# Three arms of an expert put in another order, with the group work moved into them

## The chip, the cores and the metric

The kernel runs on one core of a Trainium2 chip. The metric is the device time of one execution in microseconds (us), the median of the timed runs. Five engines run side by side, each through its own stream of instructions: PE multiplies matrices, DVE and ACT do element-wise work, POOL is little used here, and SP issues the weight transfers. Instructions stream to an engine from memory; the page lists these fetches as DMA queues of their own, of the kind "instruction".

## The reference, cut to what matters

One layer of an encoder, 256 tokens and 16 meta tokens of width 1024. A mixer (SSD and differential attention) comes first; it ends some 380 us into the execution, and the change does not touch it. Then a routed feed-forward: each of 256 tokens picks 4 of 32 experts.

```python
logits = xf @ w_router + b_router
top_val, top_idx = lax.top_k(logits, TOP_K)          # 4 of 32
gates = softmax(top_val)
# for every expert e, on the tokens that picked it:
hidden = xb @ w_gate_up[e] + b_gate_up[e]            # 1024 x 2048
gate, up = min(hidden[:D], 7), clip(hidden[D:], -7, 7)
y = gate * sigmoid(1.702 * gate) * (up + 1) @ w_down[e] + b_down[e]   # 1024 x 1024
out = segment_sum(y * gate_of_slot, slot_token)
```

Each expert has 12 MB of weights in float32, and all 32 are read: 384 MB. How many tokens an expert has depends on the data.

## The kernel before, in words

**The weight ring.** `load_page` (L1002 to L1010) brings weights in pages of 1 MB into a ring of 19 buffers (`NS`): 8 pages of `w_gate_up` and 4 of `w_down` for an expert. SP issues them. `follow(e, k)` stands behind the last use of a page and issues the page 19 places further on, so a transfer can start only when PE has done with the page in its buffer.

**An expert.** The tokens of an expert lie in slots, 32 to a part: A holds slots 0 to 31, B 32 to 63, C 64 to 95, D 96 to 127. For a part PE runs the up part (`up32`, bias at L1096, weights at L1098, into `pA` to `pD`), DVE and ACT apply the activation (`act`), PE turns the result (`turn`, L1117, `atA`), and PE runs the down part (`down32`, L1130, `dA`), whose result `place` copies to `yrow` (L1138, L1140). Parts A and B read gathered tokens from `w1`, in which four experts (a group, `GE`) lie side by side; C and D are gathered for one expert from a one-hot matrix `eo` that `pick` makes on DVE (L1045).

**The arms.** The number of tokens `n` of an expert is a register value (`counts`, L1183, loaded on each engine), and every engine branches on it. `arms` writes three arms for each of the 32 experts, unrolled: a heavy one for n > 64 (gather, A, B, and within it a further branch at L1199 on n > 96 for C alone or C and D, then `combine` into the sums `acc`, L1169), a middle one for n > 32 (A and B) and a light one (A alone). The compare is at L1192 (n > 32) and L1193 (n > 64). An engine that leaves an arm jumps over the arms behind it to the next expert; this jump is recorded with the line of its `If` (L1193 for the heavy and the middle arm).

**The hint.** `tell` marks, inside expert e, on PE alone, which way the branch labelled `x{e+1}` of the next expert will go.

**Group work.** Behind the last expert of a group, outside the arms, `gather_group` gathers the tokens of the next group into `w1` (L1055, `xg`), and for each of parts A and B `combine` adds `yrow` to the sums (L1169, `acc`) and `slots` makes the placement matrices `pgb` of the next group (L1078, L1080, `ptA` and `ptB`). All of `mark` is the start of the sums, in expert 0.

The order on PE, DVE, ACT and SP is as written (`manual_schedule`).

Of the kernel before, what the change touches and what calls it, by code (L numbers as in the profile page):

```python
# [9 lines left out]
F32 = mybir.dt.float32  # L10
# [7 lines left out]
ET = mybir.EngineType  # L18
# [29 lines left out]
def hybrid_trunk_kernel(  # L48
# [974 lines left out]
    oh = ext[:, 512:1024].rearrange("p (b s) -> p b s", b=NB)  # L1023
    bdn, yx = ext[0:NE, 1024:2048], ext[0:64, 1024:2048]
    nc.scalar.dma_start(bdn, b_down[0])
    w1 = pg.tile([128, 2, KD, 128], F32, tag="d1", name="w1")
    pgb = [[cp.tile([128, 128], F32, name=f"pgb{i}{b}", tag=t) for b, t in enumerate(ts)]
           for i, ts in enumerate((("m1", "tri"), ("pgb10", "pgb11")))]
    pgx = cp.tile([128, NB, 128], F32, tag="pb", name="pgx")[0:64]
# [8 lines left out]
                                iota[:, None, ES * i:ES * i + ES].to_broadcast([128, GE, ES]),  # L1038
                                posm[:, b, g * GE:(g + 1) * GE, None].to_broadcast([128, GE, ES]), ALU.is_equal)

    def pick(e, off, name):

        eo = wk.tile([128, NB, 64], F32, tag="sd", name=f"eo{name}")
        for b in range(NB):
            V.tensor_scalar(eo[:, b, :], iota[:, 0:64], float(off), posm[:, b, e:e + 1], ALU.add, ALU.is_equal)  # L1045
        return eo

    def gather_group(name, ks, raw=False):

# [92 lines left out]
    def ups(e, parts, last):  # L1142

        p = [wps([128, 2, 256], f"p{pt[4]}") for pt in parts]
        for k in range(KD):
            for pt, q in zip(parts, p):
                up32(e, k, weights(e, k), q, pt[0])
            if last:
                follow(e, k)
        for pt, q in zip(parts, p):  # L1150
            act(q, pt[1], wk.tile([128, 256], F32, tag="sd", name=f"th{pt[4]}"))
# [30 lines left out]
    def counts(e):  # L1182
        return nc.values_load(cnt[0:1, e:e + 1], engines=(ET.PE, ET.DVE, ET.Activation, ET.SP), min_val=0, max_val=S)  # L1183

    def arms(e, n, mark, tell):

        r0 = ES * (e % GE)
        pa = (w1[:, 0, :, r0:r0 + ES], 0, yrow[:, 0], r0, f"A{e}")
        pb_ = (w1[:, 1, :, r0:r0 + ES], 512, yrow[:, 1], r0, f"B{e}")
        pc = (xTx[:, :, 0:32], 1024, yx, 0, f"C{e}")  # L1190
        pd_ = (xTx[:, :, 32:64], 1536, yx, 32, f"D{e}")
        with tc.If(n > 32, label=f"x{e}") as c1:  # L1192
            with tc.If(n > 64) as c2:  # L1193
                eo = pick(e, 64, f"{e}")
                gather(eo, f"x{e}")
                slots(eo, slice(e, e + 1), pgx, f"x{e}")
                ups(e, [pa, pb_], False)
                tell()
                with tc.If(n > 96) as c3:  # L1199
                    ups(e, [pc, pd_], True)  # L1200
                    mark()
                    downs(e, [pa, pb_], False)
                    downs(e, [pc, pd_], True)
                with c3.Else():
                    ups(e, [pc], True)
                    mark()
                    downs(e, [pa, pb_], False)
                    downs(e, [pc], True)
                combine(pgx, yx)
            with c2.Else():  # L1210
                tell()
                ups(e, [pa, pb_], True)
                mark()
                downs(e, [pa, pb_], True)
        with c1.Else():
            tell()
            ups(e, [pa], True)
            mark()
            downs(e, [pa], True)

    front[0] = False
    for i in range(NS):
# [3 lines left out]
    with tc.manual_schedule(engines={ET.PE, ET.DVE, ET.Activation, ET.SP}):  # L1226
        gather_group("0", range(0, 8, 2), raw=True)
        cts[0] = counts(0)
        gates()
        for E, b in ((V, 0), (G, 1)):  # L1230
            E.tensor_mul(h1[:, b, :], h1[:, b, :], gb1[:, 0, :])
            E.tensor_add(h1[:, b, :], h1[:, b, :], gb1[:, 1, :])
        hd = page("d2", [2 * D], F32, "hd")
        for e in range(NE):
            g, el = divmod(e, GE)
            if e + 1 < NE:
                cts[e + 1] = counts(e + 1)
            n = cts.pop(e)
            m = cts.get(e + 1)
            if el == GE - 1 and e + 1 < NE:  # L1240
                pick_group(g + 1)
            if e + 1 == NE:
                A.activation(gsum, ident[:, 0:NB], AF.Sqrt)
                gb2 = slot[NE * PE_ % NS]
                nc.gpsimd.dma_start(gb2[:, 0, :], row_bc(ln2_g, D))  # L1245
                nc.gpsimd.dma_start(gb2[:, 1, :], row_bc(ln2_b, D))

            def mark(m=m, e=e):
                if e == 0:
                    start_acc()  # L1250
                    V.memset(yx, 0.0)

            def tell(m=m, e=e):
                if m is not None:
                    tc.mark_branch_hint_location(f"x{e + 1}", hint=m > 32, engines=[ET.PE])

            arms(e, n, mark, tell)
            if el == GE - 1 and e + 1 < NE:
                gather_group(f"{g + 1}", range(0, 8, 2))
            if el == GE - 1 and e + 1 < NE or e == 0:  # L1260
                for i in range(2):
                    if e:
                        combine(pgb[i], yrow[:, i])
                    h = g + 1 if e else 0
                    slots(oh[:, :, 128 * i:128 * i + 128], slice(h * GE, (h + 1) * GE), pgb[i], f"{'AB'[i]}{h}")
        combine(pgb[1], yrow[:, 1])


# [46 lines left out]
    with c.Else():  # L1315
        combine(pgb[0], yrow[:, 0])
        for e in range(NE):
            with tc.If(nc.values_load(cnt[0:1, e:e + 1], min_val=0, max_val=S) > 128):
                for k in range(PE_):
                    load_page(e * PE_ + k, (NE * PE_ + 1 + k) % NS)  # L1320
                for off in (128, 192):
                    nm = f"{e}o{off}"
                    eo = pick(e, off, nm)
                    gather(eo, f"x{nm}")
                    slots(eo, slice(e, e + 1), pgx, f"x{nm}")
                    p = [wps([128, 2, 256], f"p{nm}{i}") for i in range(2)]
# [49 lines left out]
```

## Time and profile before

| | us |
|---|---|
| median of 3 runs (1479.12 to 1482.28) | 1479.97 |
| the profiled execution | 1474.79 |
| its span, first to last instruction | 1472.7 |
| PE busy with matmuls | 1185.7 |
| DVE busy | 426.1 |
| ACT busy | 294.6 |

The span is given in 40 slices of 36.8 us in the page. The experts take the time from 393 to 1452 us. With this data the 32 experts take the following arms, read off the timeline of PE (L light, M middle, H heavy; a bar between groups of four):

L L L L | H L H M | M L L H | L L M L | L L L L | H L L M | L M L M | L M H L

That is 20 light ones, 7 middle ones and 5 heavy ones; one of the heavy ones (expert 11) has all four parts, the others three.

### The profile page before, as it was taken

What the parts mean: (1) busy time and instruction counts of PE and PEld (TensorE: products, weight loads), DVE (VectorE), ACT (ScalarE), POOL (GpSimd) and SP (SyncE); (2) the same over time, 40 slices, a digit from 0 to 9 for tenths busy, and PEclk for the clock granted to TensorE, in tenths of its full rate; (3) what the DMA queues carried; (4) which work ended last, traced back from release to release, by engine and by line L of the source; (5) the groups of instructions that cost most, each with busy time, mean ns of one, the idle gap of its engine ahead of it and who ended that gap; (6) DMA issues with size and microseconds to landing.
All of it is one profiled execution on the core that took longest, in us unless ns stands there. A gap on an engine that the chain in (4) does not pass through costs nothing. (4 is left out here: it accounts for less than half of the span.)

```text
span 1472.7 us, 24271 instructions
## 1 busy us (share of the span) xinstructions
PE 1185.7 (81%) x10294; PEld 727.6 (49%) x10294; DVE 426.1 (29%) x940; ACT 294.6 (20%) x630; POOL 83.0 (6%) x65
## 2 busy tenths in 40 slices
PE   5899999899777968688697976856976777787875
PEld 5799999889532533344243533411532443242432
DVE  5976765456411110211112012011021111111113
ACT  4454475454300100001000100100100010010011
POOL 5422400000100000000000000000000000000001
PEclk9999999999888999989888889977898898899888
DMA  6465673768499998877998399999998999999740
GB/s 170 133 168 125 153 185 106 225 200 332 182 405 417 418 412 354 347 301 302 377 418 325 151 416 418 415 418 418 419 382 350 416 417 416 417 416 414 307 174 31
DMA packets 101982, 458.40 MB, mean 311 GB/s; under 512 B 8626, under 2 KB 49739, under 8 KB 52635
## 3 DMA queue, kind: packets, MB, share of 16 engines
q1 hardware_dynamic: 100554, 451.59, 79.2%
q0 software_dynamic: 800, 3.03, 0.7%
q8 instruction: 146, 2.39, 0.7%
q10 hardware_dynamic: 400, 0.73, 0.2%
q14 instruction: 82, 0.66, 0.1%
HBM read 454.27 MB, written 1.05 MB: 309 GB/s over the span
## 5 line engine op out<-in xcount | busy, mean ns | idle before, releaser
L1098 PE MATMUL pA<-ring,w 128*32 128x512 f32 x2048 | 294.3, 664 | 21.7 <-DMA ring<-in_w_gate_up_dram 21.1
L1098 PEld LDWEIGHTS pA<-ring,w 128*32 128x32 f32 x2048 | 91.9, 120 | 170.9 <-issue 112.4
L1130 PE MATMUL dA<-ring,hd 128*32 128x256 f32 x2048 | 150.9, 443 | 17.4 <-ACT hd L1118 14.5
L1103 DVE TENSOR_SCALAR hd<-pA 128x256 f32<-128x256 f32 x32 | 13.6, 425 | 449.5 <-PE pA L1098 322.2
L1098 PE MATMUL pB<-ring,w 128*32 128x512 f32 x768 | 116.2, 618 | 0.0
L1130 PEld LDWEIGHTS dA<-ring,hd 128*32 128x32 f32 x2048 | 72.3, 126 | 79.8 <-issue 26.0
L1105 ACT ACTIVATE thA<-hd 128x256 f32<-128x256 f32 x32 | 13.3, 416 | 468.6 <-DVE hd L1103 455.0
L1140 DVE COPY yrow<-dA 32x256 f32<-32x256 f32 x96 | 40.4, 420 | 216.1 <-PE dA L1130 153.5
L1096 PE MATMUL pA<-bgt,sel 96*32 96x256 bf16 x256 | 19.4, 337 | 99.6 <-issue 93.2
L1096 PEld LDWEIGHTS <-sel 96*32 96x32 bf16 x400 | 12.8, 104 | 138.5 <-issue 124.5
L1055 PE MATMUL xg<-ext,hh 128*128 128x256 f32 x256 | 63.5, 410 | 8.7 <-issue 4.5
L1055 PEld LDWEIGHTS xg<-ext,hh 128*128 128x128 f32 x256 | 52.1, 206 | 21.2 <-issue 7.8
L1169 PE MATMUL acc<-yrow,pgb 128*128 128x512 f32 x128 | 58.1, 598 | 1.0 <-DVE yrow L1140 1.0
L1245 POOL DMA_DIRECT2D ring<-in_ln_g_dram x1 | 0.6, 574 | 1018.5 <-PE dB L1130 1018.5
L1098 PEld LDWEIGHTS pB<-ring,w 128*32 128x32 f32 x768 | 33.0, 116 | 46.9 <-issue 46.8
L1117 PE MATMUL atA<-ident,hd 128*128 128x128 f32 x64 | 16.0, 334 | 47.4 <-DVE hd L1111 47.4
L1138 ACT COPY yrow<-dA 32x256 f32<-32x256 f32 x32 | 11.6, 363 | 200.2 <-DVE yrow L1140 153.9
L1130 PE MATMUL dB<-ring,hd 128*32 128x256 f32 x768 | 51.6, 387 | 0.0
L1117 PEld LDWEIGHTS atA<-ident,hd 128*128 128x128 f32 x64 | 10.1, 207 | 78.2 <-issue 61.5
L1098 PE MATMUL pC<-ring,ext 128*32 128x512 f32 x320 | 39.7, 612 | 0.6 <-issue 0.6
L162 PE MATMUL xbc<-hTh,wh_xbc 128*128 128x272 f32 x128 | 38.2, 300 | 0.0
L163 PE MATMUL xbc<-hTl,wh_xbc 128*128 128x272 f32 x128 | 37.8, 296 | 0.0
(523 smaller groups left out, 2120.3 us busy)
## 6 DMA issues: line engine op xcount, KB each, us to landing
ring<-in_w_gate_up_dram SPq DMA_DIRECT2D x256, 1024.0 KB, 19.9
ring<-in_w_down_dram SPq DMA_DIRECT2D x127, 1024.0 KB, 19.5
wr_xbc<-in_w_in_dram SPq DMA_DIRECT2D x8, 1024.0 KB, 10.5
wr_g<-in_w_in_dram SPq DMA_DIRECT2D x8, 1024.0 KB
wr_z<-in_w_in_dram SPq DMA_DIRECT2D x4, 1024.0 KB
wr_k<-in_w_in_dram SPq DMA_DIRECT2D x4, 1024.0 KB, 10.9
wr_v<-in_w_in_dram SPq DMA_DIRECT2D x4, 1024.0 KB
wr_q<-in_w_in_dram SPq DMA_DIRECT2D x4, 1024.0 KB, 13.7
```

The source lines that it names most:

```text
L162: TE.matmul(p, wh, xh, start=first, stop=False)
L163: TE.matmul(p, wh, xl, start=False, stop=False)
L1055: TE.matmul(p[:, j, :], h1[:, b, k * 128:(k + 1) * 128], oh[:, b, :], start=b == 0, stop=b == 1)
L1096: TE.matmul(o[:, u, :], sel[:, e:e + 1].to_broadcast([96, 32]), bgt[u][:, 256 * j:256 * j + 256], start=u == 0, stop=False)
L1098: TE.matmul(o, x[:, k, :], w[:, :, 256 * j:256 * j + 256], start=False, stop=k == KD - 1)
L1103: V.tensor_scalar(gg, p[:, 0, :], 7.0, None, ALU.min)
L1105: A.activation(t, gg, AF.Tanh, scale=0.851)
L1117: TE.transpose(p[:, t, :], hd[:, co + 256 + t:co + 512:2], ident)
L1130: TE.matmul(p[j * 32:(j + 1) * 32, :], at[:, t, k * 32:(k + 1) * 32], w[:, t, j * 256:(j + 1) * 256], start=k == 0 and t == 0, stop=k == 3 ...
L1138: A.copy(o, p[r0:r0 + 32, :])
L1140: V.tensor_copy(o, p[j * 32:j * 32 + 32, :])
L1169: TE.matmul(ap[b][n], w[b], y[:, n * 512:(n + 1) * 512], start=False, stop=stop)
```

## The change

The light arm stands first under `If(n <= 32)`, the middle one next under `If(n <= 64)`, and the heavy one last. The hint tells `m <= 32` in place of `m > 32`. `mark` becomes `fill`, at the same place between the up and the down part; it now also holds the group work, `gather_group` in the last expert of a group, and `combine` and `slots` in the first expert of the next one. `pick(e, 64)` is called for every expert ahead of the branch, and its result `eo` lies in the page of `w1`, of which 128 elements behind the tokens are set apart.

```diff
--- before.py
+++ after.py
@@ -1023,7 +1023,9 @@
     oh = ext[:, 512:1024].rearrange("p (b s) -> p b s", b=NB)
     bdn, yx = ext[0:NE, 1024:2048], ext[0:64, 1024:2048]
     nc.scalar.dma_start(bdn, b_down[0])
-    w1 = pg.tile([128, 2, KD, 128], F32, tag="d1", name="w1")
+    w1 = pg.tile([128, KD * T], F32, tag="d1", name="w1")
+    eo = w1[:, 2 * D:2 * D + 128].rearrange("p (b s) -> p b s", b=NB)
+    w1 = w1[:, 0:2 * D].rearrange("p (i k s) -> p i k s", i=2, k=KD)
     pgb = [[cp.tile([128, 128], F32, name=f"pgb{i}{b}", tag=t) for b, t in enumerate(ts)]
            for i, ts in enumerate((("m1", "tri"), ("pgb10", "pgb11")))]
     pgx = cp.tile([128, NB, 128], F32, tag="pb", name="pgx")[0:64]
@@ -1038,12 +1040,10 @@
                                 iota[:, None, ES * i:ES * i + ES].to_broadcast([128, GE, ES]),
                                 posm[:, b, g * GE:(g + 1) * GE, None].to_broadcast([128, GE, ES]), ALU.is_equal)
 
-    def pick(e, off, name):
-
-        eo = wk.tile([128, NB, 64], F32, tag="sd", name=f"eo{name}")
+    def pick(e, off):
+
         for b in range(NB):
             V.tensor_scalar(eo[:, b, :], iota[:, 0:64], float(off), posm[:, b, e:e + 1], ALU.add, ALU.is_equal)
-        return eo
 
     def gather_group(name, ks, raw=False):
 
@@ -1182,41 +1182,41 @@
     def counts(e):
         return nc.values_load(cnt[0:1, e:e + 1], engines=(ET.PE, ET.DVE, ET.Activation, ET.SP), min_val=0, max_val=S)
 
-    def arms(e, n, mark, tell):
+    def arms(e, n, fill, tell):
 
         r0 = ES * (e % GE)
         pa = (w1[:, 0, :, r0:r0 + ES], 0, yrow[:, 0], r0, f"A{e}")
         pb_ = (w1[:, 1, :, r0:r0 + ES], 512, yrow[:, 1], r0, f"B{e}")
         pc = (xTx[:, :, 0:32], 1024, yx, 0, f"C{e}")
         pd_ = (xTx[:, :, 32:64], 1536, yx, 32, f"D{e}")
-        with tc.If(n > 32, label=f"x{e}") as c1:
-            with tc.If(n > 64) as c2:
-                eo = pick(e, 64, f"{e}")
+        pick(e, 64)
+        with tc.If(n <= 32, label=f"x{e}") as c1:
+            tell()
+            ups(e, [pa], True)
+            fill()
+            downs(e, [pa], True)
+        with c1.Else():
+            with tc.If(n <= 64) as c2:
+                tell()
+                ups(e, [pa, pb_], True)
+                fill()
+                downs(e, [pa, pb_], True)
+            with c2.Else():
                 gather(eo, f"x{e}")
                 slots(eo, slice(e, e + 1), pgx, f"x{e}")
                 ups(e, [pa, pb_], False)
                 tell()
                 with tc.If(n > 96) as c3:
                     ups(e, [pc, pd_], True)
-                    mark()
+                    fill()
                     downs(e, [pa, pb_], False)
                     downs(e, [pc, pd_], True)
                 with c3.Else():
                     ups(e, [pc], True)
-                    mark()
+                    fill()
                     downs(e, [pa, pb_], False)
                     downs(e, [pc], True)
                 combine(pgx, yx)
-            with c2.Else():
-                tell()
-                ups(e, [pa, pb_], True)
-                mark()
-                downs(e, [pa, pb_], True)
-        with c1.Else():
-            tell()
-            ups(e, [pa], True)
-            mark()
-            downs(e, [pa], True)
 
     front[0] = False
     for i in range(NS):
@@ -1245,24 +1245,23 @@
                 nc.gpsimd.dma_start(gb2[:, 0, :], row_bc(ln2_g, D))
                 nc.gpsimd.dma_start(gb2[:, 1, :], row_bc(ln2_b, D))
 
-            def mark(m=m, e=e):
+            def fill(e=e, g=g, el=el):
                 if e == 0:
                     start_acc()
                     V.memset(yx, 0.0)
+                if el == 0:
+                    for i in range(2):
+                        if e:
+                            combine(pgb[i], yrow[:, i])
+                        slots(oh[:, :, 128 * i:128 * i + 128], slice(g * GE, (g + 1) * GE), pgb[i], f"{'AB'[i]}{g}")
+                if el == GE - 1 and e + 1 < NE:
+                    gather_group(f"{g + 1}", range(0, 8, 2))
 
             def tell(m=m, e=e):
                 if m is not None:
-                    tc.mark_branch_hint_location(f"x{e + 1}", hint=m > 32, engines=[ET.PE])
-
-            arms(e, n, mark, tell)
-            if el == GE - 1 and e + 1 < NE:
-                gather_group(f"{g + 1}", range(0, 8, 2))
-            if el == GE - 1 and e + 1 < NE or e == 0:
-                for i in range(2):
-                    if e:
-                        combine(pgb[i], yrow[:, i])
-                    h = g + 1 if e else 0
-                    slots(oh[:, :, 128 * i:128 * i + 128], slice(h * GE, (h + 1) * GE), pgb[i], f"{'AB'[i]}{h}")
+                    tc.mark_branch_hint_location(f"x{e + 1}", hint=m <= 32, engines=[ET.PE])
+
+            arms(e, n, fill, tell)
         combine(pgb[1], yrow[:, 1])
 
 
@@ -1320,7 +1319,7 @@
                     load_page(e * PE_ + k, (NE * PE_ + 1 + k) % NS)
                 for off in (128, 192):
                     nm = f"{e}o{off}"
-                    eo = pick(e, off, nm)
+                    pick(e, off)
                     gather(eo, f"x{nm}")
                     slots(eo, slice(e, e + 1), pgx, f"x{nm}")
                     p = [wps([128, 2, 256], f"p{nm}{i}") for i in range(2)]
```

PE at the end of the light arm of expert 1. In these rows dA is the down part, a ring buffer holds a page, sel and bgt are the bias of the next up part, and cnt holds the token counts. Before, the light arm is the last of the three, and the load of a count (each expert loads the count of the one behind it) and the compares of expert 2 (L1192, L1193) stand right behind it, then its heavy arm:

```order
L1130 MATMUL dA_5796<-ring_3900,hd 32x256 x8
L1192 UNCONDITIONAL_BRANCH
L1183 TENSOR_LOAD cnt
L1192 COMPARE_AND_BRANCH
L1193 COMPARE_AND_BRANCH
L1070 MATMUL xgx_5855<-eo_5852,hh 128x64 x16
```

Now the same place of expert 1, the end of its light arm:

```order
L1130 MATMUL dA_5081<-ring_3900,hd 32x256 x8
L1193 UNCONDITIONAL_BRANCH
L1199 COMPARE_AND_BRANCH
L1262 REGISTER_ALU
L1371 BRANCH_PREFETCH_HINT
L1096 LDWEIGHTS sel
L1096 MATMUL pA_5126<-bgt_3324,sel 32x256
```

Behind the light arm stand now the compare that opens the other two arms (L1199) and the middle arm; the jump of L1193 leads past both to the count and the compare at which expert 2 begins.

PE at the end of the heavy arm of expert 1 (acc are the sums, pgx the placement of C and D). Before, the middle arm follows:

```order
L1169 MATMUL acc_3891<-ext,pgx 128x512
L1193 UNCONDITIONAL_BRANCH
L1255 REGISTER_ALU
L1372 BRANCH_PREFETCH_HINT
L1096 LDWEIGHTS sel
```

Now the next expert follows, with the load of a count, its one compare and its light arm:

```order
L1169 MATMUL acc_3891<-ext,pgx 128x512
L1199 UNCONDITIONAL_BRANCH
L1183 TENSOR_LOAD cnt
L1193 COMPARE_AND_BRANCH
L1262 REGISTER_ALU
L1371 BRANCH_PREFETCH_HINT
L1096 LDWEIGHTS sel
```

So the arm that ends next to the following expert is now the heavy one and no longer the light one.

PE in the light arm of expert 3, the last of the first group, between its up part (pA) and its down part (dA), as it is now:

```order
L1098 MATMUL pA_6810<-ring_3902,w_3882 32x512 x4
L1055 MATMUL xg_6865<-ext,hh 128x256 x4
L1055 MATMUL xg_6871<-ext,hh 128x256 x4
L1055 MATMUL xg_6877<-ext,hh 128x256 x4
L1055 MATMUL xg_6883<-ext,hh 128x256 x4
L1117 MATMUL atA_6889<-ident,hd 128x128 x2
```

The four rows of xg stood behind the arms before; they are now between the last up matmul and the turn, and each of the three arms holds a copy of them.

## Rows read from the trace of the kernel before

**Rows 1.** the page, whole execution: DMA rate in 40 slices, PE's code fetches

```profile
GB/s 170 133 168 125 153 185 106 225 200 332 182 405 417 418 412 354 347 301 302 377 418 325 151 416 418 415 418 418 419 382 350 416 417 416 417 416 414 307 174 31
...
q8 instruction: 146, 2.39, 0.7%
```

**Rows 2.** who PE waited for, whole execution: us in total, times, longest us

```profile
PE pA L1096 <- issue: 93.2, 16, 10.6
PE atA L1117 <- DVE hd L1111: 47.4, 26, 2.9
PE pA L1098 <- DMA ring<-in_w_gate_up_dram: 21.1, 21, 1.5
PE xgx L1070 <- DVE eo L1045: 10.4, 5, 3.1
PE atB L1117 <- DVE hd L1111: 8.0, 7, 1.5
PE pA L1096 <- DVE yrow L1140: 5.9, 4, 2.3
...
PE xg L1055 <- issue: 4.5, 2, 3.2
...
PE xg L1055 <- ACT yrow L1138: 3.1, 3, 1.0
```

**Rows 3.** timeline of PE where experts meet: start us, us, what, idle before

```profile
554.73 0.68 PE L1096 MATMUL pA<-bgt,sel 96*32 96x256 bf16 x8 [9.41 <-issue]
...
567.03 3.66 PE L1130 MATMUL dA<-ring,hd 128*32 128x256 f32 x64 [0.51 <-ACT hd L1118]
...
858.19 5.35 PE L1130 MATMUL dA<-ring,hd 128*32 128x256 f32 x64 [0.51 <-ACT hd L1118]
868.84 0.68 PE L1096 MATMUL pA<-bgt,sel 96*32 96x256 bf16 x8 [5.31 <-issue]
869.22 2.01 PE L1098 MATMUL pA<-ring,w 128*32 128x512 f32 x8
...
902.52 0.68 PE L1096 MATMUL pA<-bgt,sel 96*32 96x256 bf16 x8 [6.72 <-issue]
```

**Rows 4.** branches of PE's sequencer, single ones: ns min/median/max, start us

```profile
L1192 PEldq COMPARE_BRANCH  x1: 3577/3577/3577, 437.3 to 437.3; - x1
...
L1193 PEldq COMPARE_BRANCH  x1: 6061/6061/6061, 542.5 to 542.5; - x1
...
L1193 PEldq COMPARE_BRANCH  x1: 6257/6257/6257, 862.1 to 862.1; - x1
...
L1192 PEldq COMPARE_BRANCH  x1: 354/354/354, 1001.4 to 1001.4; - x1
...
L1193 PEldq COMPARE_BRANCH  x1: 1744/1744/1744, 1242.1 to 1242.1; - x1
...
L1192 PEldq COMPARE_BRANCH  x1: 5564/5564/5564, 1244.3 to 1244.3; - x1
...
L1193 PEldq COMPARE_BRANCH  x1: 3610/3610/3610, 1422.1 to 1422.1; - x1
```

**Rows 5.** windows around two such branches: busy by engine, PEclk, DMA share, GB/s

```profile
862.00:868.00 6.00, 1.53 (x24) 0.67 (x16) 1.26 (x3) 0.36 (x1) 0.00 (x0) 0.78 1.01 414
...
1422.00:1429.00 7.00, 2.94 (x7) 1.06 (x6) 0.03 (x1) 0.19 (x1) 0.00 (x0) 0.77 0.02 5
```

**Rows 6.** timeline of PE: starts of experts 12, 13, 19, group work behind 19

```profile
830.65 0.43 PE L1096 MATMUL pA<-bgt,sel 96*32 96x256 bf16 x8
...
847.86 0.47 PE L1096 MATMUL pA<-bgt,sel 96*32 96x256 bf16 x8 [1.51 <-DVE yrow L1140]
...
1002.21 0.38 PE L1096 MATMUL pA<-bgt,sel 96*32 96x256 bf16 x2 [0.23 <-PE dA L1130]
...
1032.62 1.56 PE L1055 MATMUL xg<-ext,hh 128*128 128x256 f32 x6
```

**Rows 7.** DVE at L1045, the one-hot of a heavy expert: ns min/median/max

```profile
L1045 DVE TENSOR_SCALAR eo<-iota,posm x10: 247/251/255, 494.0 to 1373.3; 128x64 f32<-128x64 f32 x10
```

## The prediction

> **What bounds the kernel now.** I read the page first [rows 1]: the weights stream at 412 to 419 GB/s in most slices behind the twelfth, and never faster. At 417 GB/s a page of 1.049 MB takes 2.51 us and the 12 of an expert 30.2 us. The rate falls in slices 16 to 20, 22, 23, 30, 31 and from 38 on: there the ring is full and PE is late. So PE sets the time in the neighbourhood of the heavy experts and behind the last transfer, and the stream elsewhere; a ring of 19 pages (48 us) lies between.
>
> Next, who PE waited for [rows 2]. The largest entry is not a transfer: the first bias matmul of an expert waited 93.2 us in 16 stalls on nothing that the profile shows. Second is the wait for the activation, 47.4 us in 26. The waits for weights are short, 21.1 us.
>
> The timeline shows where the 16 lie [rows 3]: where experts meet. From light to middle PE stands still for 5.31 us, from heavy to light 9.41, from middle to light 6.72. PE's branches say why [rows 4]. The compare that skips the heavy arm, 862.1, lasts 6.257 us; the jump out of the heavy arm over the middle and the light one, 542.5, 6.061; the jump of the middle arm over the light one alone, 1242.1, 1.744. Code is fetched by transfers of its own, 146 packets on q8 [rows 1]: a branch over a lot of code waits for its target. The hinted compare from light to light takes 0.354 to 3.577 us [rows 4], so a fetch that is asked for early is mostly hidden. But where a jump out of an arm lies directly ahead, the hinted compare behind it takes its full time: 5.564 us at 1244.3, and four more like it at 5.29 to 5.43 (one at 3.37, at the end). The cost hangs on the transfers: with the DMA engines at share 1.01 a far branch took 6.26 us, at 0.02 it took 3.61 [rows 4, 5].
>
> [...]
>
> **The change, part by part.** The order of the arms decides. Before, the light arm ended at the next expert and had no exit to pay; its entry was the hinted compare. Now its entry is straight on and its exit jumps over the middle and the heavy arm, the very code that the compare at 862.1 skipped. No hint names that exit: the hint names the next compare. I price the idle time of PE between experts.
>
> *One fetch.* The nearest rows are the five light-to-middle meetings, a far branch right behind a light arm: 5.31, 5.64, 5.29, 5.97, 5.70, mean 5.6 (the sequencer runs some 1.5 us ahead, so 6.2 shows as 5.6) [rows 3]. *A second fetch* right behind: 5.4, from the hinted compares behind an exit; the middle or heavy arm is now entered so. *A third*, the compare over the middle arm into the heavy one: 6.1 as the other far branches. Bounds for all three: 3.4 to 3.6 with quiet DMA engines, 6.8 (the longest L1193). I take the busy value: a light arm frees 12 pages, 30 us of transfers, in about 14 us, so its exit always meets a queue.
>
> By meeting, idle before and after:
> - light to light, 10: before 9.4 in all (2.99, the 5.9 of `yrow` [rows 2], 0.44); now 56: +46.6.
> - light to middle, 5: 27.9; now 5 x 11.0: +27.1.
> - to a heavy one from light (4) or middle (1): 10.4, the wait for `eo` [rows 2]; now 5 x 17.1: +75.1.
> - middle to light, 5: 9.12, 6.72, 6.77, and 6.6 at two where the group work lay between (2.1 of the waits of `xg` for ACT and 4.5 on nothing shown [rows 2]), 29.2; now 28: -1.2.
> - middle to middle, 1: 1.0; now 11.0: +10.
> - from heavy, 5: 9.41, 9.62, 10.63, 5.26, 0, together 34.9; now straight on, some 1.8: -33.1.
> - entry of expert 0: -2.7; exit of expert 31 with quiet engines, 3.6 less the lead: +2.5.
>
> Sum +124.3 us of PE.
>
> *Group work in the arm.* Seven light experts that begin or end a group (3, 12, 15, 16, 19, 24, 28) now fill the 2.0 us wait ahead of `atA`, four middle ones (7, 8, 23, 27) 1.1 and 1.1 ahead of `atA` and `atB` [rows 2]; the heavy ones there had their fill in C and D already. 14.0 + 8.8 = 22.8 us saved. `gather_group` is far longer than the wait, so nothing is left of it. Bound below: none, if ACT, which now copies `xg` ahead of the turn, is late.
>
> *One-hot ahead.* Two DVE instructions of 0.251 us [rows 7] for all 32 experts, hidden behind PE's exits; the 10.4 us that heavy experts waited for it are in the list. Nothing more. Without that cover it would cost 27 x 0.5 = 14 us.
>
> *What the stream gives back.* A light expert that doesn't wait for weights takes 17.2 us (847.86 less 830.65), expert 19 took 30.4 (1032.62 less 1002.21) [rows 6]; expert 18 12.9 over, 17 3.6, expert 3 some 4. That is 33 us of PE waiting for weights which a later PE swallows. I count it whole, since now PE is late everywhere: with about 35 us for an expert against the stream's 30.2.
>
> 124.3 - 22.8 - 33 = +68.5 us. The profiled execution took 1474.8 (span 1472.7), the median 1480.0 is 5.2 above it; so 1480 + 68 = 1548 us. The lower clock behind a stall (8 matmuls took 2.01 us behind the 5.31) is left out: a light expert without a stall loses as much in its down part, 5.35 for 3.66 us [rows 3]. At the worst 14 new long stalls x 1 to 1.7 us, up to 24.
>
> **Rivals.**
> 1. *The exit costs nothing* (the other side). If the target behind the arms is there in time, as the light-to-light compare nearly showed with 0.354 us, each of the 26 meetings that leave a light or a middle arm is 5.6 us cheaper: 124.3 - 145.6 - 22.8 = -44 us of PE. Where the stream binds that buys nothing; only from experts 4 to 11 and 20 to the end does it count, about half: -20, 1460 us. It decides where the exit costs under 3.0 us (5.6 less 68.5/26). Against it: five of five exits from heavy arms waited, 3.61 to 6.76 us. 11%.
> 2. *The hint holds behind the exit.* The second fetch, at 11 meetings, goes: -59, 1489 us. Against it: the six full times behind an exit [rows 4]. 8%.
> 3. *The engines are quieter than I think.* PE-bound, the stream pauses. If half of the 42 fetches cost 2.5 us less: -52, 1496; a quarter, 1522. 9%.
> 4. *Hidden.* The ring takes up a PE that is 48 us late and nothing shows: 1480 us. Against it: the end follows PE's end, and the last expert is not faster for it. 3%.
>
> **How the numbers follow.** My forecast has 69%: 1548, by its own bounds 1520 (half of the fill, the second fetch partly hinted, some quiet ones) to 1580 (clock, 6.8 for 6.1). To leave out 2 in 10 the range takes in rivals 2 and 3: 1487 to 1580. Differences under 0.2% can't be told from none. Faster: rival 1, 0.11 and a remainder of 3 and 4, 0.12; same 0.03; slower 0.85.
>
> **What would show it.** In the changed profile, `pA` at L1096 waits on nothing shown some 200 us or more in about 27 stalls. Light exits, recorded at L1193, last 5 to 7 us; the compare of the next expert lasts under 0.1 us into a light arm and above 5 into another behind an exit. Heavy to light meets without a stall. `atA`'s wait for DVE falls from 26 to about 19 times. The rate falls under 400 GB/s in slices 25 to 37 too. I am wrong if the exits at L1193 stay under 3 us, or if slices 25 to 37 keep 415 GB/s.

## The result, and the profile after

The changed kernel takes 1566.43 us (median of 4, 1559.31 to 1573.71) against 1479.55 for the kernel before: 1.0599 times as long, interval 1.053 to 1.0668, 86.9 us slower. The forecast was 1548, with 1487 to 1580 around it. The profiled execution took 1559.31 us, its span is 1557.6, PE is busy for 1179.4 us of it.

The page of the changed kernel, the same two rows as [rows 1]:

```profile
GB/s 162 130 161 119 166 171 149 151 254 335 264 390 416 256 346 305 227 392 283 380 347 217 218 415 417 417 416 417 397 299 417 416 415 403 409 336 372 202 163 31
...
q8 instruction: 171, 2.80, 0.8%
```

Who PE waited for, whole execution (columns as in [rows 2]: us in total, times, longest us):

```profile
PE pA L1096 <- issue: 156.1, 21, 11.8
PE xgx L1070 <- issue: 89.0, 5, 19.1
PE atA L1117 <- DVE hd L1111: 27.4, 15, 2.9
...
PE acc L1169 <- issue: 4.7, 1, 4.7
PE acc L1169 <- DVE ext L1140: 4.1, 4, 1.0
...
PE atB L1117 <- DVE hd L1111: 3.7, 3, 1.2
```

The two waits on nothing shown are 245.1 us in 26 stalls, where there were 93.2 in 16; the prediction had looked for all of it at `pA`, but a heavy expert's stands at its gather, `xgx`. The wait of `pA` for weights, 21.1 us before, is gone. 25 more code fetches are on q8.

PE's timeline where experts meet (columns as in [rows 3]): light to light, light to heavy, heavy to light, middle to middle, light to middle.

```profile
433.89 0.68 PE L1096 MATMUL pA<-bgt,sel 96*32 96x256 bf16 x8 [5.54 <-issue]
...
518.99 2.37 PE L1070 MATMUL xgx<-w,hh 128*128 128x64 f32 x10 [18.02 <-issue]
...
577.59 0.43 PE L1096 MATMUL pA<-bgt,sel 96*32 96x256 bf16 x8
...
706.96 0.69 PE L1096 MATMUL pA<-bgt,sel 96*32 96x256 bf16 x8 [10.61 <-issue]
...
935.44 0.68 PE L1096 MATMUL pA<-bgt,sel 96*32 96x256 bf16 x8 [11.31 <-issue]
```

One, two and three branches that wait for their code stand there as 5.5, 10.6 to 11.3 and 18.0 us, and none where a heavy arm ends. The branches behind them, as in [rows 4]: a light arm's exit, the compare into the next light arm; then the compare behind an exit and the third branch behind it; a middle arm's exit; the exit of expert 31, when the weights are all there.

```profile
L1193 PEldq COMPARE_BRANCH  x1: 6122/6122/6122, 426.8 to 426.8; - x1
...
L1193 PEldq COMPARE_BRANCH  x1: 79/79/79, 433.4 to 433.4; - x1
...
L1193 PEldq COMPARE_BRANCH  x1: 5194/5194/5194, 506.2 to 506.2; - x1
...
L1199 PEldq COMPARE_BRANCH  x1: 7355/7355/7355, 511.5 to 511.5; - x1
...
L1199 PEldq COMPARE_BRANCH  x1: 6153/6153/6153, 960.4 to 960.4; - x1
...
L1193 PEldq COMPARE_BRANCH  x1: 3498/3498/3498, 1533.1 to 1533.1; - x1
```

From one light expert to the next it is now 21.15 us (433.89 to 455.04) where [rows 6] had 17.2.

Not all of the difference lies among the experts. Expert 0's first matmul starts at 401.65 us, not at 393.01, 8.6 us later. The mixer, which the change does not touch, ends 11.2 us later, as the gather behind it shows (before, then after, with expert 0 behind it); 2.7 us of that come back because expert 0's light arm is now straight on and doesn't wait for its code:

```profile
381.68 8.64 PE L1055 MATMUL xg<-ext,hh 128*128 128x256 f32 x32 [1.06 <-DVE cmx L965]
393.01 0.42 PE L1096 MATMUL pA<-bgt,sel 96*32 96x256 bf16 x7 [2.70 <-issue]
```

```profile
392.90 8.82 PE L1055 MATMUL xg<-ext,hh 128*128 128x256 f32 x32 [1.06 <-DVE cmx L965]
401.65 0.43 PE L1096 MATMUL pA<-bgt,sel 96*32 96x256 bf16 x8
```

The stretch 0 to 380 us of before and then of after (busy time of PE, PEld, DVE, ACT, POOL; PEclk, DMA share, GB/s):

```profile
0.00:380.00 380.00, 349.74 (x2669) 327.28 (x2670) 253.58 (x471) 192.16 (x384) 73.06 (x58) 0.99 0.64 186
```

```profile
0.00:380.00 380.00, 343.25 (x2567) 323.47 (x2568) 245.76 (x440) 187.88 (x373) 72.29 (x57) 0.98 0.79 174
```

Fewer bytes, 174 GB/s for 186, keep the DMA engines busier, 0.79 for 0.64. So 8.6 us of the 84.9 between the spans lie ahead of expert 0, and 76.3 from there on.

### The profile page after: what moved, and what is told of

The parts are those of the page before. It is cut to its first block, busy times and chain, and to the rows that moved or that the text cites. A ratio compares the mean times of both kernels' runs of the same rounds, so it can differ in the third digit from the quotient of the medians.

```text
span 1557.6 us, 24393 instructions
## 1 busy us (share of the span) xinstructions
PE 1179.4 (76%) x10294; PEld 735.7 (47%) x10294; DVE 436.5 (28%) x994; ACT 294.3 (19%) x630; POOL 83.3 (5%) x65
## 3 DMA queue, kind: packets, MB, share of 16 engines
HBM read 454.27 MB, written 1.05 MB: 292 GB/s over the span
## 5 line engine op out<-in xcount | busy, mean ns | idle before, releaser
L1098 PE MATMUL pA<-ring,w 128*32 128x512 f32 x2048 | 302.2, 684 | 2.4 <-issue 2.4
L1130 PE MATMUL dA<-ring,hd 128*32 128x256 f32 x2048 | 133.6, 403 | 13.9 <-ACT hd L1118 13.9
L1070 PE MATMUL xgx<-w,hh 128*128 128x64 f32 x160 | 35.3, 422 | 89.0 <-issue 89.0
L1130 PEld LDWEIGHTS dA<-ring,hd 128*32 128x32 f32 x2048 | 66.2, 116 | 64.8 <-ACT hd L1118 18.3
L1070 PEld LDWEIGHTS xgx<-w,hh 128*128 128x128 f32 x160 | 34.5, 332 | 91.3 <-issue 91.3
L1055 PE MATMUL xg<-ext,hh 128*128 128x256 f32 x256 | 59.0, 390 | 1.1 <-DVE cmx L965 1.1
L162 PE MATMUL g<-hTh,wh_g 128*128 128x256 f32 x128 | 37.1, 290 | 3.8 <-ACT wh_g L183 3.8
L1169 PEld LDWEIGHTS acc<-yrow,pgb 128*128 128x128 f32 x128 | 23.1, 190 | 31.9 <-issue 29.3
## 6 DMA issues: line engine op xcount, KB each, us to landing
ring<-in_w_down_dram SPq DMA_DIRECT2D x127, 1024.0 KB, 11.9
```

The source lines that it names most:

```text
L162: TE.matmul(p, wh, xh, start=first, stop=False)
L1055: TE.matmul(p[:, j, :], h1[:, b, k * 128:(k + 1) * 128], oh[:, b, :], start=b == 0, stop=b == 1)
L1070: TE.matmul(p[:, k, :], h1[:, b, k * 128:(k + 1) * 128], eo[:, b, :], start=b == 0, stop=b == 1)
L1098: TE.matmul(o, x[:, k, :], w[:, :, 256 * j:256 * j + 256], start=False, stop=k == KD - 1)
L1130: TE.matmul(p[j * 32:(j + 1) * 32, :], at[:, t, k * 32:(k + 1) * 32], w[:, t, j * 256:(j + 1) * 256], start=k == 0 and t == 0, stop=k == 3 ...
L1169: TE.matmul(ap[b][n], w[b], y[:, n * 512:(n + 1) * 512], start=False, stop=stop)
```

## The experiments

Twelve kernels. The interval behind each ratio is against runs of the kernel before on the same chip (medians 1476.68 for the first four, 1481.11 for the next seven, 1480.63 for the last).

### The arms' order alone, and everything but the order

`order_only` has the three arms and the hint as after, the rest as before (the diff is cut to the compare):

```diff
-        with tc.If(n > 32, label=f"x{e}") as c1:
+        with tc.If(n <= 32, label=f"x{e}") as c1:
...
```

> The kernel before with nothing but the arms in the new order and the hint turned round; the group work stays between the experts and the one-hot inside the heavy arm. Theory (the exit of the light and the middle arm is a far branch that waits for its code): all of the loss is here. Against the changed kernel 23 us of filled waits are lost, and some 18 us come back where group work between two experts hides the second fetch: 1565 to 1580 us, light exits of 6 us. Rival (the one-hot, which now writes into the page of w1 ahead of every expert, or the group work inside the arms is what holds PE up): the time falls back to 1475 to 1490.

Measured: 1579.83 us, 1.0693 (1.0655 to 1.0731), inside its range. `work_only` is after with the order and the hint of before (cut in the same way):

```diff
-        with tc.If(n <= 32, label=f"x{e}") as c1:
+        with tc.If(n > 32, label=f"x{e}") as c1:
...
```

> The changed kernel with the arms and the hint in the order of before: group work inside the arms and the one-hot ahead of the branch stay. Theory: the loss goes. The filled waits give 23 us of PE, but at six group ends the work no longer hides the fetches behind an exit, some 22 us: 1470 to 1490 us, no difference from before. Rival (one-hot or group work cost the time): 1530 or more.

Measured: 1499.79 us, 1.0163 (1.0128 to 1.0198), above its range. So the order alone costs more than the whole change (the two intervals overlap by a hair); the group work gives some back in the new order and nothing in the old one. In the profile of `work_only` 10.9 us of the loss lie ahead of expert 0, which starts at 403.9 us. In the experts PE waits 23.5 us less for the activation, but stands 152.2 us between experts for 119.6: without group work between them more compares wait (`pA` on nothing shown 126.7 us in 19 stalls, before 93.2 in 16). `order_only` also shows what the group work hides when it stands between two branches. PE's branches at the end of expert 3, then at a light-to-heavy meeting without group work:

```profile
L1192 PEldq COMPARE_BRANCH  x1: 6154/6154/6154, 490.5 to 490.5; - x1
...
L1192 PEldq COMPARE_BRANCH  x1: 444/444/444, 509.4 to 509.4; - x1
...
L1192 PEldq COMPARE_BRANCH  x1: 5266/5266/5266, 589.0 to 589.0; - x1
```

The exit at 490.5 is followed by 17 us of group work, and the hinted compare behind it takes 0.44 us; without that work it takes 5.27.

### Does the exit's cost grow with the code that it skips?

`near_exit` is after with the heavy arm left out for the 27 experts that have no more than 64 tokens with this data; with other data it would compute them wrongly. A light exit then skips one middle arm, and a middle arm has no exit. (The diff is cut to the branch.)

```diff
-            with tc.If(n <= 64) as c2:
+            if e in (4, 6, 11, 20, 30):
+                heavy(e, n, pa, pb_, pc, pd_, fill, tell)
+            else:
                 tell()
                 ups(e, [pa, pb_], True)
```

> The changed kernel with the heavy arm left out of the 27 experts that do not need it with this data, so that a light arm skips the middle arm alone (twice the code that the middle arm skipped before, for 0.3 to 4.2 us) and a middle arm ends next to the following expert. Theory (a target not yet fetched costs one whole fetch, however far it is): light exits stay at 6 us; the middle exits and what hangs on them go, about 45 us of PE, 1515 to 1535 us. Rival (the wait grows with the code that is skipped): light exits fall to 2 us or less, 1450 to 1485 us.

Measured: 1538.15 us, 1.0399 (1.0358 to 1.0439), 3 us above its range. The light exits stay where they were: 18 of 20 take 5.92 to 7.11 us, expert 0's 4.62 and expert 31's, at the end, 3.68. Expert 1's, over one middle arm:

```profile
L1193 PEldq COMPARE_BRANCH  x1: 6320/6320/6320, 450.0 to 450.0; - x1
```

What is bought is the exit of the middle arms: middle to light 5.7 us in five meetings instead of 33.0. Over one arm the jump costs what it costs over two: the rival falls for these two distances. It is no rule for every distance: before, the jump of a middle arm over the light arm alone took 0.34 to 4.24 us (seven cases, one of them in [rows 4]).

### Is the hint lost behind an exit?

`common_tail` has before's order, but the down part of A and the gather of the next group stand once, behind the three arms, so that some 4 to 7 us of PE's work lie between an exit and the next compare. (The one-hot is ahead of the branch and in the page of `w1`, `start_acc` ahead of expert 0, the other group work inside the arms. The diff is cut to the light arm.)

```diff
         with c1.Else():
             tell()
             ups(e, [pa], True)
-            mark()
-            downs(e, [pa], True)
+            early()
+        late()
+        downs(e, [pa], True)
```

> Arms in the order of before, light last; the down part of A, which all three arms have, stands once behind the arms, the gather of the next group with it. Theory (a hinted compare behind an exit pays because nothing lies between; work between exit and compare hides the fetch): compares at L1193's outer level behind a middle or heavy arm fall from 5.4 to under 1 us, against 7 us more wait for the activation in middle arms: 1440 to 1470 us, faster than before. Rival (the hint is dropped by the exit itself): these compares stay at 5 us, 1470 to 1490 us.

Measured: 1503.18 us, 1.017 (1.0114 to 1.0226): the time missed, the mechanism held in most cases. The exit of expert 20's heavy arm and the hinted compare behind the tail, and under it who PE waited for:

```profile
L1194 PEldq COMPARE_BRANCH  x1: 5957/5957/5957, 1123.4 to 1123.4; - x1
...
L1193 PEldq COMPARE_BRANCH  x1: 386/386/386, 1135.4 to 1135.4; - x1
```

```profile
PE atB L1117 <- DVE hd L1111: 16.2, 6, 2.7
PE xgx L1070 <- DVE w L1046: 11.1, 5, 3.1
...
PE acc L1169 <- DVE ext L1140: 8.7, 5, 2.5
PE atA L1117 <- DVE yrow L1140: 7.8, 4, 2.0
```

The hint holds over the exit, but here it mostly helped with 5.6 us or more of other work in between, and not with 3.9. Of the four compares behind a heavy arm's exit that lead to a light arm, three take 0.39 to 0.40 us, 5.6 us or more behind that exit; expert 5's, 3.9 us behind it, still takes 6.76. Two of the five behind a middle arm take 4.1 us, which stays open. The idle time of PE behind heavy arms fell from 42.2 to 11.0 us and from middle to light from 29.2 to 6.8, and between experts in all from 119.6 to 76.3. But all idle time of PE from expert 0 on fell only from 238.4 to 230.6: part of the stalls now stands ahead of the turn (6.8 us), and the waits shown here grew. PE's busy time there grew by 12.5 us, and expert 0 starts 25.8 us later, with `start_acc` and a later mixer ahead of it.

### Why does the mixer end later?

All kernels so far with `eo` in the page of `w1` were slow in the mixer, the two without it (before and `order_only`) were not. But their programs also differ in length. Three kernels tell these apart. `w1_only` is before with that tile edit alone, `before_pad` before with code that never runs, `after_own` after without the tile edit and the one-hot ahead; their edits, in this order and cut to the main lines:

```diff
-    w1 = pg.tile([128, 2, KD, 128], F32, tag="d1", name="w1")
+    w1 = pg.tile([128, KD * T], F32, tag="d1", name="w1")
+    eo = w1[:, 2 * D:2 * D + 128].rearrange("p (b s) -> p b s", b=NB)
```

```diff
                     combine(pgx, yx)
+                    combine(pgx, yx)
+                    combine(pgx, yx)
         for t in pgx:
```

```diff
-        pick(e, 64)
...
+                eo = pick(e, 64, f"{e}")
```

> The kernel before with one edit alone: `eo` lies in the page of `w1` (`w1` becomes a tile of KD x T elements, of which `eo` is a view); arms, hint, group work and the place of `pick` stay as before. In the runs so far, every kernel with this edit reached expert 0's compare some 7 to 11 us later than the kernels without it, and the 1 KB packets of the mixer's weights lasted 89 ns on average against 63 to 64. Theory (the tile edit does it): compare of expert 0 at 397 to 402 us, DMA share of 0:380 near 0.79, mean 1 KB packet near 89 ns, and 1484 to 1492 us in all. Rival (the length of the programs does it, since order_only is the only other kernel with programs as long as before's): compare at 388 to 394, share 0.64, and the time of before, 1477 within 4 us.

> The kernel before with two more `combine` calls for each of the 32 experts in the branch for experts of over 128 tokens, behind all of the work, which this data never takes: some 500 more instructions on PE that nothing executes, and nothing else. Theory (tile edit): nothing changes, compare of expert 0 at 388 to 394 us, share of 0:380 0.64, 1477 within 4 us. Rival (length of the programs, by where they and the weights then lie in memory): compare at 397 to 402, share near 0.79, 1484 to 1492 us.

> The kernel after without the one-hot edit: `pick` is back inside the heavy arm and `eo` back in its own work tile, `w1` as before; arms, hint and group work as after. Theory (tile edit): the mixer ends 7 to 11 us earlier, compare of expert 0 at 388 to 394, share of 0:380 0.64; of that, heavy arms give back up to 2 us each, unless DVE makes `eo` while PE still stands in its third fetch. 1554 to 1562 us. Rival (length of the programs): compare at 397 to 402 and 1564 to 1570 us. By the prediction's step on the one-hot (10.4 us of heavy arms' waits for it were in the list of meetings) the waits of `xgx` for DVE come back at up to 10 us; if the third fetch covers them they stay under 3.

Measured: `w1_only` 1478.91 us, 0.9983 (0.9963 to 1.0004); `before_pad` 1492.05, 1.0075 (1.0047 to 1.0103); `after_own` 1568.65, 1.0585 (1.0554 to 1.0616). My theory fell. `before_pad`, whose added lines stand in a branch behind all of the work, starts expert 0 at 406.1 us; its stretch 0 to 380, and under it that of `w1_only`, taken on the same chip:

```profile
0.00:380.00 380.00, 345.62 (x2560) 325.02 (x2561) 245.42 (x439) 187.95 (x373) 72.14 (x57) 0.97 0.78 173
```

```profile
0.00:380.00 380.00, 350.20 (x2674) 327.67 (x2674) 254.24 (x471) 192.78 (x384) 73.09 (x58) 0.99 0.64 187
```

With the tile edit alone, expert 0 starts at 392.4 and the share is 0.64. So it is not the tile edit, and code that is never executed is enough to slow the mixer. To see whether longer is always slower I took ten extra calls in place of two:

```diff
-                    combine(pgx, yx)
+                    for _ in range(11):
+                        combine(pgx, yx)
```

> before_pad with ten extra `combine` calls for an expert in place of two: 2560 matmuls that nothing executes, in place of 512. Theory (where the program and the weights lie in memory, by its length, decides how fast the 1 KB packets are; no rule that longer is slower, since near_exit is a third shorter than before and slow): the mean of the 1 KB packets and the mixer's end fall anywhere between the two cases seen, 63 and 89 ns, 388 and 402 us. Rival (longer is slower): 89 ns or more, compare of expert 0 at 402 or later, 1492 us or more.

Measured: 1489.65 us, 1.0067 (1.0038 to 1.0097), share 0.76, expert 0 at 406.6. The mean 1 KB packet took 86.9 ns, not more than the 88.9 with two calls. With a program a third shorter (`near_exit`) the share was 0.78, with hints and short branches added (`hint_mid`, below) 0.68. Longer is not the rule; that it is where program and weights come to lie in memory was my guess, and no run shows it.

`after_own` settles the one-hot as well: without it the time is the same, and no wait of `xgx` for `eo` returns: all of its waits, 88.0 us in five, are on nothing shown. The prediction had the one-hot cost nothing because it would be made in that time; inside the heavy arm it costs nothing either.

### Hints for the other branches

If a fetch asked for early is hidden, the compare that skips the heavy arm should take a hint too. `hint_inner` is before with that:

```diff
-            with tc.If(n > 64) as c2:
+            with tc.If(n > 64, label=f"y{e}") as c2:
...
+                    tc.mark_branch_hint_location(f"y{e + 1}", hint=(m + 223) % 256 > 31, engines=[ET.PE])
                     tc.mark_branch_hint_location(f"x{e + 1}", hint=m > 32, engines=[ET.PE])
```

> The kernel before with one addition: the inner compare (n > 64) gets a label and a hint of its own on PE, given just ahead of the hint of the outer one, and worked out so that it says 'jump' for a middle expert alone. Theory (a far branch costs a fetch, and one asked for a light arm's length earlier is mostly hidden): the compare that skips the heavy arm behind a light arm falls from 5.3 to 6.3 us to 0.4 to 3.6 at the five light-to-middle meetings, the rest stays; 15 to 25 us of PE less, of which the stream leaves half to all: 1455 to 1470 us. Rival (only one hint is held, and the one given last takes its place): the inner compares stay at 5 to 6 us, 1474 to 1484 us. Second rival (a hint costs, or disturbs the outer one): light-to-light compares rise to 5 us and the time to 1500 and above.

Measured: 1487.08 us, 1.0034 (1.0011 to 1.0057). Light to middle stayed (30.2 us in five): the first rival, with a time 3 us above its range. `hint_mid` gives the inner hint last, and only ahead of a middle expert:

```diff
                     tc.mark_branch_hint_location(f"x{e + 1}", hint=m > 32, engines=[ET.PE])
+                    with tc.If((m + 223) % 256 < 32):
+                        tc.mark_branch_hint_location(f"y{e + 1}", hint=m > 64, engines=[ET.PE])
```

> The kernel before with a hint for the inner compare that is given behind the outer one's, and only where the next expert is a middle one: a short branch on the count skips it otherwise, so the last hint that PE meets is always the one whose jump will be taken. In hint_inner the hint of the inner compare stood ahead of the outer one's and changed nothing (6.0 to 6.5 us behind a light arm). Theory (only the last hint is held): the five compares that skip the heavy arm behind a light arm fall to 0.4 to 3.6 us, light to light stays as before; 13 to 25 us of PE less, 1458 to 1472 us, or some 11 more where the program's new length slows the mixer's packets (share of 0:380 near 0.79), 1469 to 1483. Rival (a hint reaches only the next compare, not the one behind it): these five stay at 5 to 6.5 us, and the time at 1478 to 1494.

Measured: 1498.09 us, 1.0147 (1.0095 to 1.0198). Expert 23's compare over its heavy arm in `hint_inner`, and then in `hint_mid`, with the exit of that middle arm:

```profile
L1193 PEldq COMPARE_BRANCH  x1: 6162/6162/6162, 1162.9 to 1162.9; - x1
```

```profile
L1193 PEldq COMPARE_BRANCH  x1: 378/378/378, 1164.9 to 1164.9; - x1
...
L1193 PEldq COMPARE_BRANCH  x1: 5619/5619/5619, 1196.3 to 1196.3; - x1
```

The mechanism is right: light to middle falls to 11.9 us in five, though one compare of the five still takes 5.0. The time isn't: part of it comes back at the middle arms' exits (26.0 us in seven, 11.3 before), and a short branch of some 0.25 us is added for nearly every expert. Of the 19.0 us between the profiles' spans 4.7 lie ahead of expert 0; from there on PE is idle for 8.3 us more and busy for 5.9 us more. `hint_all` adds a hint for the compare on n > 96 (cut to the main lines):

```diff
+                ups(e, [pa, pb_], False,
+                    lambda: tc.mark_branch_hint_location(f"z{e}", hint=n > 96, engines=[ET.PE]))
+                with tc.If(n > 96, label=f"z{e}") as c3:
+                    tell()
```

> hint_mid, and a hint of its own for the compare on n > 96 inside the heavy arm, given three pages ahead of it; the hints for the next expert move behind that compare, into its two arms. By the theory the compare on n > 96 of the four heavy experts with three parts falls from 3.4 to 6.3 us (19.5 in the sum of before) to under 3.6, some 10 to 16 us of PE less than hint_mid, 5 to 15 of the time: 1450 to 1468 (1461 to 1479 with a slow mixer). Rival: the hint is given too near, or the pages that PE reads straight on take its place: the compares stay above 5 us and the time is that of hint_mid within 4 us.

Measured: 1468.72 us, 0.9917 (0.9886 to 0.9948): faster than the kernel before, by 12.4 us, and inside the range given for a slow mixer (expert 0 starts at 404.0). To see which hint does it, `hint_c3` is before with the four lines above and no inner hint.

> The kernel before with the hint for the compare on n > 96 alone, three pages ahead of it in the heavy arm, and the next expert's hint moved behind that compare; no hint for the inner compare and no extra branch. hint_all was 12 us faster than before, though in its profile the mixer ended 11 us later; hint_mid, the same without this hint, was 17 us slower than before. Theory (this hint carries the gain: a fetch asked for where the arm then reads straight on costs nothing later): the compares on n > 96 of experts 4, 6, 20 and 30 fall from 19.5 us together to under 8, light to middle stays at 6, and with a program of before's length the mixer stays at 0.64 to 0.66: 1455 to 1469 us. Rival (the gain of hint_all needs the hint of the inner compare too): 1470 to 1481 us. Second rival (the gain was one of place in memory): the compares fall, and the time is before's, or above.

Measured: 1481.08 us, 0.9996 (0.9967 to 1.0025). The four compares fell as expected (6.08, 3.30, 6.19 and 3.38 before, 6.2 together now), and the time did not: my theory fell. PE stands 108.1 us between experts in `hint_all`, 114.4 in `hint_mid`, 123.5 in `hint_c3` and 119.6 before. Between experts alone these stalls do not order the times, 1469, 1498 and 1481 us and 1481 before. All of PE's stalls on nothing shown from expert 0 on do, those inside heavy arms and around the group work included: 85.3 us in 18 for `hint_all`, 107.6 in 22 before, 110.3 in 21 for `hint_c3` and 114.9 in 27 for `hint_mid`. So a hint alone moves its stall to other places: `hint_mid` has 9.3 us of it ahead of `xg` (4.5 before) and 7.4 ahead of `acc` (3.9 before), and `hint_c3` has 101.0 ahead of `pA` (91.0 before). Why these other stalls stay away with both hints is open.

## Why the prediction was right

**The bound and the mechanism.** An exit over two arms waits for its code, every time: the 19 light exits ahead of expert 31 last 5.93 to 6.57 us, the compare behind them 0.07 into a light arm and 5.2 to 6.3 into another, and four of five heavy arms end without a stall for code. In the trace of after a packet of q8 (16 KB, 1.07 us at the median) starts within each of PE's 49 branches of over 0.6 us, and within none of its 30 shorter ones. In `near_exit` 18 of 20 exits over one arm take as long, 5.92 to 7.11 us. Rival 1 would have needed exits under 3.0 us, which only expert 31's nears (3.50). Rival 2 (the hint holds behind the exit) is half true, as `common_tail` shows: it holds, but too late to be of use here. Far compares with a hint came down to 0.38 us (`hint_mid`) and 0.39 (`common_tail`).

**The sum, term by term.** Idle time of PE between the last matmul of an expert's down part and the first of the next up part (gaps over 0.25 us, group work taken out), by meeting; forecast is what the prediction's list gives for the changed kernel:

| meeting | forecast | measured |
|---|---|---|
| light to light, 10 | 56 | 56.1 |
| light to middle, 5 | 55 | 56.3 |
| to a heavy one, 5 | 85.5 | 89.0 |
| middle to light, 5 | 28 | 33.0 |
| middle to middle, 1 | 11 | 10.6 |
| from a heavy one, 5 | 1.8 | 8.8 |

Counted the same way PE stood 119.6 us before and 253.9 now: +134.3, forecast +124.3 (of which -0.2 are expert 0's entry and expert 31's exit, not counted here). The largest term that was too small is **middle to light**, by 5.0 us, of which one meeting makes 4:

```profile
1389.86 0.68 PE L1096 MATMUL pA<-bgt,sel 96*32 96x256 bf16 x8 [9.82 <-issue]
```

The exit ahead of it takes 6.56 us and the compare of expert 28, at 1385.61, 0.07; then PE stands for some 4 us more, straight on and on nothing shown, which stays open. Next is the **third fetch**, by 3.5: 7.35 to 7.51 us in four of five, for 6.1. From a heavy arm the two errors cancel. Four meetings wait 1.0 us for the copy ahead of `combine` and the fifth 4.7 for the exit out of the arm for n > 96; the list left these out of both sides, for they stood before too:

```profile
PE acc L1169 <- DVE ext L1140: 4.1, 4, 1.0
PE acc L1169 <- issue: 3.9, 1, 3.9
```

Heavy arms' ends went from 42.2 to 8.8 us, -33.4 where the forecast was -33.1.

**Group work in the arm.** The waits for the activation fell by 20.0 us at `atA` and 4.3 at `atB`; forecast 22.8. `atA` waits 15 times where there were 26, for the 11 experts that the sum counts; the sign said about 19 and had left out its four middle ones.

**The clock, left out.** It cost about what the bound said (18.8 of up to 24 us), and most of it was given back. PE's groups from 395 us on, before and then after (busy us, mean ns; idle before):

```profile
L1098 PE MATMUL pA<-ring,w 128*32 128x512 f32 x2042 | 293.3, 664 | 21.7 <-DMA ring<-in_w_gate_up_dram 21.1 <-issue 0.6
L1130 PE MATMUL dA<-ring,hd 128*32 128x256 f32 x2048 | 150.9, 443 | 17.4 <-ACT hd L1118 14.5 <-DMA ring<-in_w_down_dram 2.9
...
L1070 PE MATMUL xgx<-eo,hh 128*128 128x64 f32 x160 | 24.4, 325 | 10.4 <-DVE eo L1045 10.4
```

```profile
L1098 PE MATMUL pA<-ring,w 128*32 128x512 f32 x2048 | 302.2, 684 | 2.4 <-issue 2.4
L1130 PE MATMUL dA<-ring,hd 128*32 128x256 f32 x2048 | 133.6, 403 | 13.9 <-ACT hd L1118 13.9
...
L1070 PE MATMUL xgx<-w,hh 128*128 128x64 f32 x160 | 35.3, 422 | 89.0 <-issue 89.0
```

Matmuls behind a stall got slower (`pA` +7.9 with the six matmuls of before that lie ahead of 395 us, 294.3 in all; `xgx` +10.9 us), and those of the down part faster (`dA` -17.3). Expert 1 shows the first: the granted clock is at 0.50 of full speed from 430.4 us, in the stall, to 437.3, and at 1.00 from there to 454. The prediction put the second down to the stall; it is not the stall's doing. In `order_only`, with the same stalls and the group work outside, `dA` takes 149.3 us, and in `work_only`, with the old order, 135.6. In the seven light experts with group work ahead of the down part `dA` takes 3.66 us in after and in `work_only`, and 5.05 to 5.35 in six of them in `order_only`. With two middle ones that makes 12.6 of the 17.3 us. In the other light experts `dA` varies between 3.66 and 6.3 us, and what decides there is not shown.

**The stream gives back.** Expert 19 took 53.4 us from its first matmul to the first of expert 20's up part, and takes 51.3 with an 18.3 us stall in it; 8.3 of the 53.4 were sums and placement matrices that now lie inside expert 20. The experts' stretch grew by 76.3 us for 134.3 of idle time: 58.0 came back, forecast 22.8 + 33 = 55.8. That the two agree so well is in part luck. What came back is 24.3 us of waits for the activation, 24.0 of waits for weights (21.1 at `pA` and 2.9 at `dA`, all that there were), and 8.6 by which PE's busy time from expert 0 on fell, which the forecast had at nothing. The 33 were lengths of whole experts, of which waits for weights were only a part: expert 19 was 13.2 us over, with 8.2 us of such waits. One sign was wrong: the rate doesn't fall under 400 GB/s all through slices 25 to 37, only in slices 29, 30, 36 and 37 and behind. A row of light experts at 21 us each still uses pages faster than the 30.2 us that the stream takes for them, so it works at its bound to refill the ring, late PE or not (415 to 417 GB/s in slices 24 to 28).

**What was missing.** The sum of +68.5 us was made over the experts, where 76.3 was measured; the excess is idle time between experts, 9.8 us more than forecast when meetings alone are counted, less the 2.2 that came back on top. The step that failed is that the mixer adds nothing: expert 0 started 8.6 us later in the profile, and code that never runs cost 11 us by itself (`before_pad`). The range was drawn upwards for the clock and for longer exits; that a later mixer fell inside it too is luck.

## What to carry to other kernels

Write last, or straight on, the path that is taken most often, and count a jump out of each other arm as a whole fetch (5.93 to 6.57 us here with the DMA engines at a share of 0.97 to 1.05, 3.50 at 0.02), over one middle arm as over two arms; over a light arm alone it was 0.34 to 4.24. In the one pair of hints tried only the last one given was of use, and behind a far jump a hint mostly helped with 5.6 us or more of other work in between, and not with 3.9. A gain at one branch has to be looked for in the sum of all stalls: a single hint moved them. And before a small difference is put down to an edit, see whether a stretch that the edit doesn't touch has moved too: a kernel with code that never runs is the control.

## What was not expected of the hardware

Code that is never executed made the weight transfers of the mixer slower: with 512 more matmuls on PE, each with its weight load, behind the end of the work the DMA share from 0 to 380 us rose from 0.64 to 0.78, the mean of the 1 KB packets (worked out from the trace's packets ahead of expert 0) from 63 to 89 ns, and the time by 0.75%. `w1_only`, taken on the same chip, has 64.5 ns. The effect does not grow with the length (86.9 ns with 2560 more), and its cause stays open.
